# The cross stage's LayerNorm and the third quarter of the mix, turned by DMA in 16-bit planes

## The chip, the cores and the metric

One core of one Trainium2 chip. The metric is the device time of one execution in microseconds; the median of the runs counts. The engines are named as in the profile: PE (TensorE), DVE (VectorE), ACT (ScalarE), POOL (GpSimd) and SP (SyncE, which issues most DMAs). Each engine works through its own queue in order.

## The reference, cut to what matters

One layer of an encoder block over 256 tokens of width 2048, all in float32: a SwiGLU feed-forward, a mixer with two attentions, a cross attention to 256 memory tokens, and a second feed-forward, each followed by a LayerNorm. The change lies between the mixer's output and the cross attention's queries:

```python
# in the mixer: y_a, y_b are the two attentions' outputs, g_a and g_b the gates
return (g_a * y_a + g_b * y_b) @ w_out
# in the layer
h = layer_norm(ALPHA * h + mix, ln_mix_g[l], ln_mix_b[l])
xa = memory_cross_attention(h, mem, mem_ln_g[l], mem_ln_b[l], w_xq[l], w_xkv[l], w_xo[l])
h = layer_norm(ALPHA * h + xa, ln_x_g[l], ln_x_b[l])
# in memory_cross_attention
m = layer_norm(mem, mem_ln_g, mem_ln_b)
q = (h @ w_xq).reshape(b, s, X_HEADS, X_HEAD_DIM)
kv = (m @ w_xkv).reshape(b, m_len, 2, X_HEADS, X_HEAD_DIM)
```

## The kernel before

The 256 tokens are two token tiles of 128 (tt 0 and 1). Activations that enter a matmul are kept transposed, with the features on the partitions, as two halves: a high part (a copy rounded to the format that PE multiplies fast, fp32r) and a low part (the rest). `Act` holds them in blocks of 512 features, a "quarter" each. A product is computed as high x high + high x low + low x high.

Weights come in tiles of 1 MB. SP loads one into a `raw` buffer (three of them, L191); ACT casts its high part in two pieces (L262), DVE takes the low part (L265); two pairs of such buffers (`hi`, `lo`) are filled in turn while PE works on the other. A raw buffer is free again when its low part is taken. `run` writes this out: ahead of each item of the program it forms the tiles of the items to come, and `weave` puts side items (functions that form, send or join something) in front of given main items. A scheduler then places the instructions of each engine in one fixed order.

There are two ways to turn a [tokens x 512 features] piece.

- On PE: four transposes by the identity into PSUM (L417 in `ln_T`, L1301 in the mix).
- By DMA in 16-bit planes: `planes` (L840, ACT) separates the upper and lower 16 bits of each word into two planes, `send` (L844, SP) transposes both by one DMA, `join` (L848, ACT) puts the words together again. `issue_after` binds a send behind the last weight load issued, and a weight load behind the last send.

After either, `split` forms the high part (L253, ACT) and the low part (L254, DVE).

The stages around the change, in order:

- **w_o_b**, second half: `out_b(1)` multiplies by the gates and adds the two branches (L1275 to L1277, DVE), features 1024 to 1535 first (n = 0, the mix's third quarter), then 1536 to 2047 (n = 1, the fourth).
- **w_out**, two groups of eight steps. Step c (counted from 1 in this text) reads features 256(c-1) to 256c-1, so the third quarter is first read by the fifth step, the fourth by the seventh. PE does 24 matmuls of width 512 a step. Beside it runs `mem_norm`, the memory's LayerNorm: statistics on DVE (L387 to L399), a spread by eight small matmuls (L1365), and four quarters.
- **Cross stage, keys**: eight keys, one 1 MB tile each: 16 matmuls of width 512 (L275) and 16 of 256 (L277); ACT and DVE add and split the result (L283, L284, L253, L254). Beside them the LayerNorm of h: `ln_scale`, then `ln_T` on the quarters: scaling (L409 on DVE, L411 on ACT), four PE transposes, gain and bias out of PSUM (L424 on ACT, L426 on DVE), split.
- **Cross stage, queries**: two groups of eight steps over the same h, quarter 0 in steps 1 and 2, both token tiles in each step; the fifth and seventh steps of the first group work on sums of blocks (`forms_step`, `Sums`), whose weights use the blocks X2 and X3.

Of the kernel before, what the change touches and what calls it, by code (L numbers as in the profile page):

```python
# [13 lines left out]
AF = mybir.ActivationFunctionType  # L14
ALU = mybir.AluOpType
# [3 lines left out]
P = 128  # L19
# [80 lines left out]
class Kernel:  # L100
# [738 lines left out]
    def planes(self, s, u, n):  # L839
        return self.nc.scalar.copy(self.words(u, n).rearrange("p (k c) -> p k c", k=2),  # L840
                                   self.words(s, n).rearrange("p (c k) -> p k c", k=2))

    def send(self, s, u, n):
        return self.nc.sync.dma_start_transpose(self.words(s, n).rearrange("p (b q) -> p b q", q=P), self.words(u, n))  # L844

    def join(self, s, u, n, behind=None):
        with self.tc.issue_after((behind or self.next_hi).ins):
            self.nc.scalar.copy(self.words(u, n).rearrange("p (c k) -> p k c", k=2),  # L848
                                self.words(s, n).rearrange("p (k c) -> p k c", k=2))
# [14 lines left out]
    def mixer(self, xT, st, steps):  # L864
        nc, t = self.nc, self.t
        SPANS = ((0, P), (P, 3 * P))
        e = self.__dict__
# [26 lines left out]
        a, b, c = steps(1)  # L894
# [6 lines left out]
        bias = {}  # L901
# [303 lines left out]
        for i in range(NA):  # L1205
            side = [[lat_send(0)], [], [lat_join(0)], [lat_join(1)]][2 * i:2 * i + 2] if i < 2 else ([], [])
# [42 lines left out]
        n = B_HEADS - 1  # L1249
# [17 lines left out]
        def out_b(g):  # L1267
            ps, qs = {}, {}

            def done():  # L1270
                for n in range(2):
                    v = gates[2 * g + n]
                    for tt in range(2):
                        s = qs["add"][tt, n]
                        nc.vector.tensor_tensor(s, s, ps[tt, n], ALU.add)  # L1275
                        nc.vector.tensor_tensor(v[:, tt, 1, :], v[:, tt, 1, :], s, ALU.mult)
                    nc.vector.tensor_tensor(v[:, :, 1, :], v[:, :, 1, :], v[:, :, 0, :], ALU.add)  # L1277
                    if g == 0 or n:
                        for tt in range(2):
                            self.planes(v[:, tt, 1, :], v[:, tt, 0, :], 512)  # L1280

            def send(n):
                def fn():
                    for tt in range(2):
                        v = gates[2 * g + n][:, tt]
                        with self.tc.issue_after(self.last_load.ins):
                            self.sent = self.send(v[:, 1, :], v[:, 0, :], 512)
                return fn

            def turn(n, sent=True):  # L1290
                def fn():
                    mix.blocks += self.act([("X0", "X1", "T0", "X3")[2 * g + n]]).blocks
                    for tt in range(2):
                        v = gates[2 * g + n][:, tt]
                        if sent:
                            self.join(v[:, 1, :], v[:, 0, :], 512)
                            p = v[:, 0, :]
                        else:
                            p = self.group_tile(g)
                            for j in range(4):  # L1300
                                nc.tensor.transpose(p[:, j * P:(j + 1) * P], v[:, 1, j * P:(j + 1) * P], self.ident)  # L1301
                        hi, lo = (mix.blk(a, 8 * g + 4 * n, 4)[:, :, tt * P:(tt + 1) * P] for a in (0, 1))
                        self.split(p.rearrange("p (j q) -> p j q", j=4), hi, lo)
                return fn
            self.pair_group(g, t["w_o_b"][g], 512, KT, lambda: oB["t"], AT_YB[g], fb, ps, qs, None,
                            (("H5", "X2"), "X3"))
            self.add(done, prio=SOON)
            if g:
                return {2: [turn(0, False)], 3: [send(1)], 5: [turn(1)]}
            return {2: [send(0)], 4: [send(1)], 5: [turn(0)], 6: [turn(1)]}  # L1310

        main = self.collect(lambda: out_a(0))
# [4 lines left out]
        side = out_b(0)  # L1317
# [7 lines left out]
        side = self.mem_norm()  # L1325
# [54 lines left out]

        return {0: [load], 3: [stat], 7: [spread], 8: [quarter(0)], 10: [quarter(1)], 12: [quarter(2)], 14: [quarter(3)]}

    def cross(self, xT, st, steps, steps_out):
# [115 lines left out]
        form_q = lambda c: self.forms_step(fq, SUMS_XQ, c, xT)  # L1499
# [16 lines left out]
        a, b = steps(0), steps(1)  # L1516
        group(keys, {0: a[0] + b[0], 2: a[1], 4: a[2], 6: b[1], 8: b[2]}, 0, 8)
        side = group(query, {1: [form_q(4)], 3: [form_q(6)], 6: [form_q(2)]}, 0)
        side = group(query, both(side, {4: [form_v(2)]}), 1)
        group(val, both(side, {2: [form_v(4)], 4: [form_v(6)]}), 0)  # L1520
        group(keys, {0: [ready(0)], 2: [scores(0), gb(0)], 3: [send(0), ready(1)], 4: [gb(1)], 5: [join(0), scores(1)],
# [40 lines left out]
    def build(self):  # L1562
        self.setup()
        xT0, ps0 = self.start()
        x = {"T": xT0}
        xT = lambda: x["T"]
        st = [None, None]
        ln = [self.ln_steps(n, st, x) for n in ("ln_ffn1", "ln_mix", "ln_x")]
        self.ffn("ffn1", xT, st, ps0, ln[0], tags=(
            ("T0", "T1", "early"), ("T2", "T3", "early"), ("X0", "X1", "early"), ("X2", "X3", "early")))  # L1570
        self.mixer(xT, st, ln[0])
        self.cross(xT, st, ln[1], ln[2])
        load, fin = self.final_steps(st)
# [124 lines left out]
```

## Time and profile before

| | |
|---|---|
| runs, median (lowest, highest) | 2436.84 us (2436.31, 2438.87) |
| the profiled execution | 2436.7 us, its span 2434.9 us |
| granted PE clock, mean | 0.999 |
| PE busy | 99% of the span |
| DMA | 513.57 MB, mean 211 GB/s |

A row of the page or of the timeline names start and length in us, the engine, the line, the operation, out<-in with sizes, the count, and in brackets how long the engine had been idle and for whom. In the windows, each engine's busy time and count stand in the order PE, PE weight load, DVE, ACT, POOL, then the granted clock, the DMA share and GB/s. Grouped rows end in total busy time, mean ns of one, idle time ahead and who ended it. DMA rows end in the time from issue to landing.

### The profile page before, as it was taken

The page shows a single profiled execution, that of the slowest core. Times are in us where ns is not written, and L with a number is a line of the kernel's source. Part 1 is how long each engine was busy: PE and PEld are TensorE (multiplying, and loading weights), DVE is VectorE, ACT ScalarE, POOL GpSimd, SP SyncE. Part 2 cuts the span into 40 slices and gives each one's busy share as a digit, 9 for nine tenths or more (in the row PEclk, how much of TensorE's full clock was granted, in tenths as well). Part 3 has the DMA queues.
Part 4 walks back from the last instruction along what each step waited for, and adds up shares of the span by engine and source line. Part 5 has one row for each costly group of instructions (what it writes and reads, how often), then busy time and mean ns, then how long its engine had stood idle before and what let it go on. Part 6 is the DMA issues. An engine that isn't in the chain of part 4 may idle for free.

```text
span 2434.9 us, 29728 instructions
## 1 busy us (share of the span) xinstructions
PE 2420.7 (99%) x11314; PEld 2024.9 (83%) x11314; DVE 2120.0 (87%) x2428; ACT 1534.3 (63%) x2002; POOL 38.9 (2%) x83
## 2 busy tenths in 40 slices
PE   9999999999999999999999999999999999999998
PEld 8888888888888888888888888888888888888886
DVE  8999989899878897789789888879879999898996
ACT  6676745666555557878565667665666675557662
POOL 0000000000000001000000000000000000000000
PEclk9999999999999999999999999999999999999999
DMA  7766656667655657776576557655556666666664
GB/s 268 252 214 215 208 199 218 213 198 222 228 176 206 212 210 241 235 202 175 188 256 230 190 190 209 214 185 190 188 200 217 227 221 208 223 209 206 205 215 174
DMA packets 165854, 513.57 MB, mean 211 GB/s; under 512 B 101168, under 2 KB 101936, under 8 KB 110544
## 3 DMA queue, kind: packets, MB, share of 16 engines
q1 hardware_dynamic: 160256, 493.20, 61.0%
q0 software_dynamic: 4592, 17.30, 2.2%
q8 instruction: 88, 1.44, 0.2%
q10 hardware_dynamic: 864, 1.18, 0.1%
q14 instruction: 54, 0.44, 0.1%
HBM read 485.30 MB, written 2.10 MB: 200 GB/s over the span
## 4 chain that ended last, share of the span: by engine, by line
PE 91%; DVE 4%; ACT 3%; DMA 1%; issue 1%; SPq 0%; DVEq 0%; ACTq 0%
PE at L309 25%; PE mm L309 25%; PE at L363 11%; PE mm L363 11%; PE mm L296 10%; PE mm L275 5%; PE mm L277 2%; DVE lo L265 2%; ACT hi L262 1%; PE at L1027 1%; DMA raw<-w_xv 0%; PE at L417 0%; DMA raw<-w_xq 0%; PE at L1081 0%; ACT H L848 0%
## 5 line engine op out<-in xcount | busy, mean ns | idle before, releaser
L262 ACT CAST hi<-raw 128x1024 fp32r<-128x1024 f32 (+1 forms) x852 | 805.1, 982 | 473.8 <-PE at L309 160.2
L265 DVE TENSOR_TENSOR lo<-raw,hi 128x2048 fp32r<-128x2048 f32 (+1 forms) x427 | 902.2, 2114 | 139.6 <-ACT hi L262 134.4
L309 PE MATMUL mm<-hi,T 128*128 128x512 f32 (+1 forms) x1328 | 310.7, 383 | 0.2 <-ACT hi L253 0.2
L309 PEld LDWEIGHTS mm<-hi,T 128*128 128x128 f32 x1328 | 247.1, 188 | 47.1 <-ACT hi L253 0.7
L262 ACT CAST X<-H 128x1024 fp32r<-128x1024 f32 (+1 forms) x170 | 175.0, 1035 | 162.7 <-DVE H L246 126.2
L309 PE MATMUL at<-hi,T 128*128 128x512 f32 x1152 | 275.5, 389 | 0.0
L309 PEld LDWEIGHTS at<-hi,T 128*128 128x128 f32 x1152 | 216.2, 188 | 45.1
L265 DVE TENSOR_TENSOR X<-H,X 128x2048 fp32r<-128x2048 f32 (+1 forms) x85 | 191.4, 2251 | 66.3 <-ACT X L262 65.2
L309 PE MATMUL mm<-lo,T 128*128 128x512 f32 (+1 forms) x664 | 160.4, 382 | 0.0
L309 PEld LDWEIGHTS mm<-lo,T 128*128 128x128 f32 x664 | 123.7, 188 | 22.8
L309 PE MATMUL at<-lo,T 128*128 128x512 f32 x576 | 142.4, 389 | 0.0
L309 PE MATMUL at<-hi,H 128*128 128x512 f32 x560 | 133.7, 389 | 0.0
L309 PEld LDWEIGHTS at<-lo,T 128*128 128x128 f32 x576 | 108.1, 188 | 22.5
L309 PEld LDWEIGHTS at<-hi,H 128*128 128x128 f32 x560 | 104.9, 188 | 21.5
L248 DVE TENSOR_TENSOR H<-H,raw 128x512 f32<-128x512 f32 (+1 forms) x170 | 115.1, 677 | 2.2
L309 PE MATMUL mm<-hi,H 128*128 128x512 f32 x480 | 115.2, 391 | 0.1
L246 DVE TENSOR_TENSOR H<-raw 128x1024 f32<-128x1024 f32 (+1 forms) x85 | 101.9, 1199 | 4.8 <-DMA raw<-w_gate 4.4
L309 PEld LDWEIGHTS mm<-hi,H 128*128 128x128 f32 x480 | 89.6, 188 | 18.8 <-DVE w L284 0.5
L363 PE MATMUL mm<-X,X 128*128 128x512 f32 x342 | 91.1, 392 | 0.0
L363 PE MATMUL at<-X,X 128*128 128x512 f32 (+1 forms) x315 | 82.3, 385 | 0.4 <-ACT X L262 0.4
L262 ACT CAST X<-raw 128x1024 fp32r<-128x1024 f32 (+1 forms) x50 | 51.1, 1034 | 45.5 <-DVE raw L248 34.7
L848 ACT COPY w<-w 128x1024 uint16<-128x1024 uint16 (+1 forms) x60 | 75.7, 1275 | 1.4 <-DMA w<-w 1.4
(355 smaller groups left out, 4098.0 us busy)
## 6 DMA issues: line engine op xcount, KB each, us to landing
raw<-ffn_w_in SPq DMA_DIRECT2D x150, 1024.0 KB, 4.8
raw<-ffn_w_out SPq DMA_DIRECT2D x66, 1024.0 KB, 4.9
raw<-w_gate SPq DMA_DIRECT2D x32, 1024.0 KB, 4.9
raw<-ffn_w_out_r SPq DMA_DIRECT2D x16, 1024.0 KB, 5.0
raw<-w_qk SPq DMA_DIRECT2D x16, 1024.0 KB, 5.4
raw<-w_o_b SPq DMA_DIRECT2D x16, 1024.0 KB, 4.8
raw<-w_out SPq DMA_DIRECT2D x16, 1024.0 KB, 4.8
raw<-w_xk SPq DMA_DIRECT2D x16, 1024.0 KB, 4.9
```

What stands on the lines that cost most here:

```text
L246: self.nc.vector.tensor_tensor(two[0], two[1], raw[:, :m].unsqueeze(1).to_broadcast([P, 2, m]), ALU.add)
L248: self.nc.vector.tensor_tensor(t[:, a * m:a * m + m], t[:, b * m:b * m + m], raw[:, a * m:a * m + m], ALU.add)
L262: self.last_hi = self.nc.scalar.copy(hi[:, c:d], src[:, c:d])
L265: self.last_lo = self.nc.vector.tensor_tensor(lo[:, :n], src, hi[:, :n].bitcast(F32), ALU.subtract)
L275: self.nc.tensor.matmul(ps, hi[j], x.both(kt), start=(j == 0), stop=False)
L277: self.last_mm = self.nc.tensor.matmul(ps[:, :S], lo[j], x.at(0, kt), start=False, stop=(j == n - 1))
L296: self.last_mm = self.nc.tensor.matmul(ps, x.at(xi, kt)[:, tt * P:(tt + 1) * P], w[wi][:, j * 512 + c:j * 512 + c + m], start=(start and j ...
L309: self.last_mm = self.nc.tensor.matmul(ps[tt, g][:, :n], x.at(xi, kt)[:, tt * P:(tt + 1) * P], w[wi][:, c:c + n], start=first and j + wi + ...
L363: self.last_mm = self.nc.tensor.matmul(bank[:, :m], a[xi], v[wi][:, c * m:(c + 1) * m], start=own and first and wi + xi == 0, stop=own and ...
L848: self.nc.scalar.copy(self.words(u, n).rearrange("p (c k) -> p k c", k=2), self.words(s, n).rearrange("p (k c) -> p k c", k=2))
L1027: nc.tensor.matmul(ps[:, c0:c0 + nk], q[:, tt * P:(tt + 1) * P], k[:, :nk], start=(j == 0), stop=(j == len(parts) - 1))
```

## The change

The third quarter of the mix no longer goes through PE: `planes`, `send`, `join` and `split` serve all four quarters. The cross stage's LayerNorm no longer uses `ln_steps`; a new `turned_norm` gives four kinds of steps (scale, planes, send, join), which are spread over the eight keys and the first steps of the first query group. Its planes live in the blocks X2, X3, H5 and X2 again.

```diff
@@ out_b, done
-                    if g == 0 or n:
-                        for tt in range(2):
-                            self.planes(v[:, tt, 1, :], v[:, tt, 0, :], 512)
+                    for tt in range(2):
+                        self.planes(v[:, tt, 1, :], v[:, tt, 0, :], 512)
@@ out_b, turn
-                        if sent:
-                            self.join(v[:, 1, :], v[:, 0, :], 512)
-                            p = v[:, 0, :]
-                        else:
-                            p = self.group_tile(g)
-                            for j in range(4):
-                                nc.tensor.transpose(p[:, j * P:(j + 1) * P], v[:, 1, j * P:(j + 1) * P], self.ident)
+                        self.join(v[:, 1, :], v[:, 0, :], 512)
...
             if g:
-                return {2: [turn(0, False)], 3: [send(1)], 5: [turn(1)]}
+                return {1: [send(0)], 3: [turn(0), send(1)], 5: [turn(1)]}
@@
+    def turned_norm(self, ln, st, x):
+        nc, e, got = self.nc, {}, {}
+        def scale(tt):
+            def fn():
+                if tt == 0:
+                    x["T"] = self.act(["T0", "T1", "T2", "T3"])
+                got[tt] = self.ln_scale(st[tt])
+            return fn
+        def planes(tt, q):
+            def fn():
+                if q % 2 == 0:
+                    e[tt, q // 2] = self.block(("X2", "X3", "H5", "X2")[2 * tt + q // 2], (P, 2, 2, 512))
+                mean, r, nb = got[tt]
+                hs = self.h[tt][:, q * 512:(q + 1) * 512]
+                nc.vector.tensor_scalar(hs, hs, mean, r, ALU.subtract, ALU.mult)
+                self.planes(hs, e[tt, q // 2][:, q % 2, 0, :], 512)
+            return fn
+        def send(tt, q):
+            def fn():
+                v = e[tt, q // 2][:, q % 2]
+                with self.tc.issue_after(self.last_load.ins):
+                    self.sent = self.send(v[:, 1, :], v[:, 0, :], 512)
+            return fn
+        def join(tt, q):
+            def fn():
+                v = e[tt, q // 2][:, q % 2]
+                self.join(v[:, 1, :], v[:, 0, :], 512)
+                f, a = (v[:, i, :].rearrange("p (j c) -> p j c", j=4) for i in range(2))
+                for j in range(4):
+                    kt = 4 * q + j
+                    g, b = self.vec(ln + "_g", kt), self.vec(ln + "_b", kt)
+                    if j % 2 == 0:
+                        nc.scalar.activation(a[:, j], f[:, j], AF.Identity, bias=b, scale=g)
+                    else:
+                        nc.vector.tensor_scalar(a[:, j], f[:, j], g, b, ALU.mult, ALU.add)
+                self.split(a, *(x["T"].blk(s, 4 * q, 4)[:, :, tt * P:(tt + 1) * P] for s in (0, 1)))
+            return fn
+        return scale, planes, send, join
@@ cross
-        a, b = steps(0), steps(1)
-        group(keys, {0: a[0] + b[0], 2: a[1], 4: a[2], 6: b[1], 8: b[2]}, 0, 8)
-        side = group(query, {1: [form_q(4)], 3: [form_q(6)], 6: [form_q(2)]}, 0)
+        scale, planes, nsend, njoin = norm
+        group(keys, {0: [scale(0), scale(1)], 1: [planes(0, 0), planes(0, 1)], 2: [nsend(0, 0), nsend(0, 1), planes(0, 2)],
+                     3: [planes(0, 3), nsend(0, 2), njoin(0, 0)], 4: [nsend(0, 3), njoin(0, 1), planes(1, 0)],
+                     5: [planes(1, 1), nsend(1, 0), njoin(0, 2)], 6: [nsend(1, 1), njoin(0, 3), planes(1, 2)],
+                     7: [planes(1, 3), nsend(1, 2), njoin(1, 0)], 8: [nsend(1, 3), njoin(1, 1)]}, 0, 8)
+        side = group(query, {1: [njoin(1, 2)], 2: [form_q(4), njoin(1, 3)], 4: [form_q(6)], 6: [form_q(2)]}, 0)
@@ build
-        self.cross(xT, st, ln[1], ln[2])
+        self.cross(xT, st, self.turned_norm("ln_mix", st, x), ln[2])
```

How it moves the instructions is seen at three places. The first is DVE at the start of w_out. `lo` with its buffers is a weight's low part (the last one shown is that of w_out's fifth step, loaded into raw_10382 before and raw_10371 now), BN_STATS and BN_AGGR are the memory's statistics, and the L254 on a T block is the third quarter's low part. Before:

```order
L265 TENSOR_TENSOR lo_10339<-raw_10336,hi_10338 128x2048
L254 TENSOR_TENSOR T_1626_10343<-at_10344,T_1626_10343 128x4x128
L254 TENSOR_TENSOR T_1626_10343<-at_10351,T_1626_10343 128x4x128
L265 TENSOR_TENSOR lo_10385<-raw_10382,hi_10384 128x2048
L387 BN_STATS bn_10392<-T_1612_10269 128x6 x4
L387 BN_STATS bn_10415<-T_1613_10270 128x6
```

Now, to the first token tile's low part:

```order
L265 TENSOR_TENSOR lo_10374<-raw_10371,hi_10373 128x2048
L387 BN_STATS bn_10381<-T_1612_10271 128x6 x4
L387 BN_STATS bn_10404<-T_1613_10272 128x6
L392 BN_AGGR mv_10386<-bn_10381 128x2
...
L387 BN_STATS bn_10404<-T_1613_10272 128x6
L375 TENSOR_SCALAR a_10389<-y_10388,v_10387 128x1
L392 BN_AGGR mv_10409<-bn_10404 128x2
L254 TENSOR_TENSOR T_1647_10431<-H_970_6445,T_1647_10431 128x4x128
```

The quarter's low parts moved from ahead of the fifth step's low weight to behind it and behind all eight statistics.

The second is SP from the third key's load on. Before, the loads of keys (w_xk) and queries (w_xq) follow one another:

```order
L191 DMA raw_10986<-w_xk 128x2048
L191 DMA raw_11031<-w_xk 128x2048
L191 DMA raw_11106<-w_xk 128x2048
L191 DMA raw_11151<-w_xk 128x2048
L191 DMA raw_11223<-w_xk 128x2048
L191 DMA raw_11268<-w_xk 128x2048
```

Now:

```order
L191 DMA raw_11036<-w_xk 128x2048
L844 DMA_TRANSPOSE X_1716_10993<-X_1716_10993 128x8x128 x2
L191 DMA raw_11086<-w_xk 128x2048
L844 DMA_TRANSPOSE X_1722_11045<-X_1722_11045 128x8x128
L191 DMA raw_11141<-w_xk 128x2048
L844 DMA_TRANSPOSE X_1722_11045<-X_1722_11045 128x8x128
L191 DMA raw_11198<-w_xk 128x2048
L844 DMA_TRANSPOSE H_1733_11156<-H_1733_11156 128x8x128
L191 DMA raw_11253<-w_xk 128x2048
```

Two transposes stand ahead of the fifth key's load (raw_11086), one ahead of each load after it.

The third is PE at the first query step, whose first token tile goes to the banks mm_11379 and mm_11380, the second to mm_11381 and mm_11382; T_1696 is quarter 0. Before (mm_11417 and mm_11418 are the first token tile's banks, the other two the second's):

```order
L417 MATMUL at_11405<-ident,h_102 128x128 x4
L309 MATMUL mm_11417<-hi_11341,T_1719_11038 128x512 [waits Activation_49]
L309 MATMUL mm_11417<-hi_11341,T_1719_11038 128x512
L309 MATMUL mm_11418<-hi_11341,T_1719_11038 128x512 [waits DVE_49,PE_49]
L309 MATMUL mm_11418<-hi_11341,T_1719_11038 128x512
L309 MATMUL mm_11419<-hi_11341,T_1719_11038 128x512 [waits DVE_49]
```

Now:

```order
L309 MATMUL mm_11379<-hi_11311,T_1696_10911 128x512 [waits Activation_49]
L309 MATMUL mm_11379<-hi_11311,T_1696_10911 128x512
L309 MATMUL mm_11380<-hi_11311,T_1696_10911 128x512 [waits PE_49]
L309 MATMUL mm_11380<-hi_11311,T_1696_10911 128x512
L309 MATMUL mm_11379<-hi_11311,T_1696_10911 128x512 [waits Activation_49]
L309 MATMUL mm_11379<-hi_11311,T_1696_10911 128x512
L309 MATMUL mm_11380<-hi_11311,T_1696_10911 128x512
L309 MATMUL mm_11381<-hi_11311,T_1696_10911 128x512 [waits Activation_49]
```

Seven matmuls of the first token tile now stand ahead of the first one of the second, which waits for ACT; the LayerNorm's transposes are gone. On ACT the joins of the second token tile's first two quarters stand together behind the last plane copy, then the last key's total (L283), then the split of quarter 0.

More of the change, by code (lines that the diff above doesn't have):

```diff
@@ L1288, in send, with turn @@
                 return fn
-            def turn(n, sent=True):
+            def turn(n):
                 def fn():
@@ L1294, in fn @@
                         v = gates[2 * g + n][:, tt]
-                        if sent:
-                            self.join(v[:, 1, :], v[:, 0, :], 512)
-                            p = v[:, 0, :]
-                        else:
-                            p = self.group_tile(g)
-                            for j in range(4):
-                                nc.tensor.transpose(p[:, j * P:(j + 1) * P], v[:, 1, j * P:(j + 1) * P], self.ident)
+                        self.join(v[:, 1, :], v[:, 0, :], 512)
                         hi, lo = (mix.blk(a, 8 * g + 4 * n, 4)[:, :, tt * P:(tt + 1) * P] for a in (0, 1))
-                        self.split(p.rearrange("p (j q) -> p j q", j=4), hi, lo)
+                        self.split(v[:, 0, :].rearrange("p (j q) -> p j q", j=4), hi, lo)
                 return fn
@@ L1381, in mem_norm, with cross @@
         return {0: [load], 3: [stat], 7: [spread], 8: [quarter(0)], 10: [quarter(1)], 12: [quarter(2)], 14: [quarter(3)]}
-    def cross(self, xT, st, steps, steps_out):
+    def turned_norm(self, ln, st, x):
[36 more added lines that the diff above has]
+        return scale, planes, send, join
+    def cross(self, xT, st, norm, steps_out):
         nc, t, e = self.nc, self.t, self.mem
```

## The prediction

> **What bounds the kernel now.** The first view is the page's busy shares and the chain that ended last.
>
> ```profile
> PE 2420.7 (99%) x11314; PEld 2024.9 (83%) x11314; DVE 2120.0 (87%) x2428; ACT 1534.3 (63%) x2002; POOL 38.9 (2%) x83
> PE 91%; DVE 4%; ACT 3%; DMA 1%; issue 1%; SPq 0%; DVEq 0%; ACTq 0%
> ```
>
> TensorE is busy for 2420.7 of 2434.9 us. Every matmul removed there is worth its length, as long as nothing else makes TensorE wait; every wait that is added counts in full. The second view is the windows over the two stages that the change touches, the start of w_out and the first eight keys of the cross stage.
>
> ```profile
> 1290.00:1330.00 40.00, 40.00 (x186) 33.33 (x185) 34.81 (x54) 21.05 (x24) 0.00 (x0) 1.00 0.68 217
> 1374.00:1422.00 48.00, 47.97 (x289) 42.48 (x287) 39.77 (x74) 31.50 (x55) 0.00 (x0) 1.00 0.52 178
> ```
>
> TensorE (first column) never stops in either. VectorE works 87% and 83% of them, ScalarE 53% and 66%. So there is room on ScalarE, but not much on VectorE. The third view is the chain in order of time, where the transposes stand among the matmuls.
>
> ```profile
> 1285.06 10.88 PE mm L309 x48
> 1295.94 0.87 PE at L1301 x8
> 1296.82 27.23 PE mm L309 x120
> ...
> 1373.91 3.63 PE mm L275 x16
> 1377.54 1.91 PE mm L277 x16
> ...
> 1385.02 0.44 PE at L417 x4
> ...
> 1385.96 0.66 PE at L417 x4
> ...
> 1397.30 0.87 PE at L417 x8
> ...
> 1421.33 0.87 PE at L417 x8
> 1422.21 21.81 PE mm L309 x96
> ```
>
> A 512-wide matmul takes 27.23/120 = 0.227 us, a w_out step of 24 of them 5.44, a key 3.65 + 1.92 = 5.57.
>
> **What leaves.** The mix's eight transposes: 0.87 us. The LayerNorm's 32: without them the first query step would start at 1373.91 + 8 x 5.57 = 1418.47 instead of 1422.21, so 3.74 us. Together 4.61 us, or 2432.1 against the profiled execution's 2436.7, if nothing waits. (That execution's span is 2434.9; the median of the runs is 2436.8, so differences carry over with +0.1.)
>
> **The mix's third quarter.** It now goes through ScalarE (two plane copies), SP (two transposes), ScalarE (two joins, two splits) and VectorE (two low parts). The rows of w_out's first half:
>
> ```profile
> 1295.86 1.21 DVE L1277 TENSOR_TENSOR H<-H 128x1024 f32<-128x1024 f32 x1
> 1302.59 2.29 DVE L265 TENSOR_TENSOR lo<-raw,hi 128x2048 fp32r<-128x2048 f32 x1 [1.67 <-ACT hi L262]
> 1304.80 3.06 DVE L387 BATCH_NORM_STATS2 bn<-T 128x6 f32<-128x512 f32 x5
> 1310.38 2.23 DVE L265 TENSOR_TENSOR lo<-raw,hi 128x2048 fp32r<-128x2048 f32 x1
> 1313.15 0.68 DVE L254 TENSOR_TENSOR X<-H,X 128x512 fp32r<-128x512 f32 x1
> 1297.11 2.00 ACT L840 COPY H<-H 128x1024 uint16<-128x1024 uint16 x2 [0.94 <-DVE H L1277]
> 1299.01 1.07 ACT L253 CAST T<-at 128x512 fp32r<-128x512 f32 x2
> 1308.98 2.56 ACT L848 COPY H<-H 128x1024 uint16<-128x1024 uint16 x2
> 1311.41 1.13 ACT L253 CAST X<-H 128x512 fp32r<-128x512 f32 x2
> 1312.45 2.00 ACT L262 CAST hi<-raw 128x1024 fp32r<-128x1024 f32 x2
> ```
>
> From start to start a plane copy costs ScalarE 0.95 us, a join 1.22, a split 0.52, a weight tile 1.9. VectorE's low part of a weight costs 2.2.
>
> The order on VectorE is what decides. Before, the third quarter's low parts stood ahead of the low weights of w_out's fifth step and of the memory's statistics (L387 to L392). Now they stand behind both. I follow that piece. The fourth quarter's plane copies start when L1277 ends, at 1297.1, and end at 1299.0; that VectorE chain is unbroken and unmoved. The fourth step's weight tile, which used to be cast ahead of them, now follows them: 1300.9. Then the first join, 1302.1, and the fifth step's weight tile, 1304.0. VectorE takes that tile's low part until 1306.3, then the eight statistics with their small steps, which before ran from 1304.80 to 1310.38, 5.58 us: 1311.9. Only then comes the quarter's first low part, 0.6: 1312.5. TensorE reaches the fifth step at 1307.70 - 0.87 = 1306.83, has four matmuls that need the high part only (0.9), and waits from 1307.7 to 1312.5, 4.8 us. Before, it stood at that point at 1308.6. Net +3.9; one of the spread's eight matmuls (0.1) is pulled into the gap: **+3.8 us** for this half. What it rests on: the weights must be there. In the queue the fourth and fifth steps' loads now stand behind two transposes; those can start at 1290.8 (planes behind the first half of a weight tile), leave SP at 1293.3, and a load behind two transposes took this long:
>
> ```profile
> 1298.18 2.72 SPq L844 DMA_TRANSPOSE H<-H  x2
> raw<-w_out SPq DMA_DIRECT2D x1, 1024.0 KB, 6.0
> ```
>
> That gives 1299.3 for the fourth step's tile and about 2 us more for the fifth's, just ahead of their casts. Bounds for this half: +3.4 (no join ahead of the tile) to +6 (the loads 2 us later). Nothing is late behind it: the sixth step's tile lands by 1309, its low part is done at 1316.3, and TensorE wants it at 1316.8 + 3.6.
>
> **The LayerNorm.** Each of eight quarters is now scaled on VectorE alone (L409's op; the four L411 on ScalarE go), copied to planes, sent, joined, multiplied by gain and bias from SBUF instead of PSUM, and split. ScalarE gains 8 x (0.95 + 1.22) and loses 4 x 0.7: +14.6 us in a stretch where it had 16.5 us free, and it takes its queue in order. So I add up that queue as the order gives it.
>
> ```profile
> 1383.19 2.00 ACT L262 CAST hi<-raw 128x1024 fp32r<-128x1024 f32 x2 [1.97 <-PE mm L275]
> 1385.09 0.81 ACT L411 ACTIVATE h<-h,nb,y 128x512 f32<-128x512 f32 x1
> L283 ACT COPY w<-mm 128x256 f32<-128x256 f32 x69 | 24.6, 367 | 9.1 <-PE mm L277 9.0
> L253 ACT CAST X<-w 128x256 fp32r<-128x256 f32 x16 | 6.5, 405 | 17.0 <-DVE w L284 17.0
> L424 ACT ACTIVATE w<-at,vecs 128x128 f32<-128x128 f32 x48 | 20.6, 456 | 5.2 <-PE at L417 4.1 <-DVE w L426 0.6
> w<-w SPq DMA_TRANSPOSE x60, 3.1
> 1469.28 5.27 DMA raw<-w_xq
> ```
>
> (Times on the clock of before.) ScalarE is free for the first planes at 1385.1; the copy ends at 1386.1, the transpose lands 3.1 us later, and the first join starts at 1389.3, ScalarE having waited 1.9 us for it. From there to the split that completes quarter 0 of the second token tile stand six joins (7.3), six plane copies (5.7), five weight tiles (9.5), six key totals and six key splits (0.3 each with the 0.1 by which neighbours overlap: 3.5), twelve gain-and-bias steps (0.36: 4.3) and five splits (2.6): 32.9 us, so 1422.2. Two things lengthen it. The load of the fifth key's tile stands behind two transposes, leaves at 1388.8 and takes 5.3: 1394.1, 0.4 us late for ScalarE; the next tile waits a little too. And a step that reads what the step ahead of it wrote loses some 0.1. I add 1.6: 1423.8. TensorE ends the keys at 1418.47, has seven matmuls of the first token tile to do (1.6: 1420.0), and then waits **3.8 us** for that split. Bounds: 2 (no waits) to 7. The keys themselves get through: the fifth key's first half tile is ready at 1395.1, wanted at 1396.2. VectorE's part lies beside this, its low part 0.7 us after the split, under four matmuls. At no cost I put the four scalings that move to VectorE (0.5 each, in 8 us of free time there; without that room they would delay the low weights by 2) and the ten further transfers (256 KB each, at a DMA share of 0.52 in this window). Later quarters are joined at 1430 and 1431 and wanted four steps on. Net for the LayerNorm: 3.8 - 3.74 = **+0.1**.
>
> One rule speaks against the change. The rows give 0.87 us for eight transposes on TensorE and 3.1 for a whole transfer, eight blocks of 128x128 in 16 bits. The Trainium skill ("VectorE: DVE Perf Modes", section "The three transpose paths") puts one such block at 1309 ns by DMA and 390 ns on TensorE and advises TensorE where PSUM will do. Eight blocks end to end would be, as an estimate from that page, 10.5 us a transfer, and the first join 7 us later; the trace's 3.1 does not agree, so the sum goes by the row.
>
> **The sum:** +3.8 + 0.1 = 3.9; 2436.8 + 3.9 = **2440.7 us**, 0.16% slower, which counts as no change (0.2%, 4.9 us, is about what can be told here).
>
> **The rivals.** (B) *Transposes land late between loads*: on the slower side.
>
> ```profile
> H<-H SPq DMA_TRANSPOSE x6, 7.8
> ```
>
> In the mix stage transposes set between loads took 7.8 us; in the key stage each now stands between two loads. If the first took that, the first join and all behind it come 4.7 us later, first as a wait at the fifth key (tile ready at about 1399.8 instead of 1396.2), the rest at the query: 2440.7 + 4.7 = 2445.4. It decides from 1.0 us of lateness on (2441.7). Against it: the queue is empty when the first one goes. (C) *ScalarE keeps up*: its bursts have slack, the LayerNorm's 3.74 come in whole, and only the mix's wait stays: 2436.8 + 3.8 - 3.7 = 2436.9. Against it the 32.9 us above. (D) *Both are hidden*: 2432.2; it needs the statistics done 5 us sooner in the mix, and the order sets them behind a low weight that cannot start before 1304.0. (E) *The wait costs clock*:
>
> ```profile
> 2418.12 5.03 PE L296 MATMUL mm<-X,H 128*128 128x512 f32 x30
> 2427.50:2428.00 0.50, 0.00 (x0) 0.00 (x0) 0.50 (x1) 0.00 (x0) 0.50 (x2) 0.91 0.00 0
> 2428.00:2429.00 1.00, 0.00 (x0) 0.00 (x0) 1.00 (x2) 0.00 (x0) 1.00 (x2) 0.50 0.00 0
> ```
>
> After the last matmul (2423.2) the granted clock holds 4.7 us and then falls to 0.50. A wait as long, followed by the fifth step's last 20 matmuls at half speed, costs 20 x 0.227 = 4.5 us: 2445.2. The spread's matmul breaks this wait in two, which speaks against it. The Trainium skill ("TensorE: Matmul & The Clock Gate", section "What's actually happening") has the clock halve after one idle window of about 3.4 us; by that rule the second wait (3.8) could do it too, and the trace agrees that some such limit exists.
>
> **How the numbers follow.** A 0.50 (its own range 2438.5 to 2443, of which 0.13 lies over 2441.7), B 0.27, C 0.13, D 0.06 (0.04 of it faster), E 0.04. Slower 0.13 + 0.27 + 0.04 = 0.44, faster 0.04, the same 0.52. The range takes in C below and most of B and E above: 2434.5 to 2447.5.
>
> **What would show it.** TensorE's busy time falls by 4.6 to about 2416, its idle time grows by some 8.5. In w_out's fifth step TensorE waits 4 to 5 us for VectorE's L254, right behind the statistics; at the first query step 2 to 5 us for ScalarE's L253. ScalarE is over 85% busy between the first planes and the query. I am wrong if the fifth step of w_out shows no wait, if the keys wait for weights, or if a transpose of the key stage lands in over 5 us.

## The result, and the profile after

| | before | after |
|---|---|---|
| runs, median (lowest, highest) | 2436.95 us (2436.31, 2438.87) | 2446.92 us (2444.71, 2450.21) |
| the profiled execution, its span | 2436.7, 2434.9 us | 2444.71, 2442.8 us |
| granted PE clock, mean | 0.999 | 0.996 |

The ratio is 1.0039, with a 95% interval of 1.0029 to 1.005: slower, by more than the 0.2% that can be told. The forecast of 2440.7 us was 6.2 us too low.

The page after the change, its busy shares and its chain:

```profile
PE 2421.1 (99%) x11274; PEld 2023.7 (83%) x11274; DVE 2121.4 (87%) x2432; ACT 1553.4 (64%) x2018; POOL 38.8 (2%) x83
PE 94%; ACT 2%; DVE 1%; DMA 1%; issue 1%; SPq 0%; DVEq 0%; ACTq 0%
```

The forty transposes are gone (11314 instructions before, 11274 now), yet TensorE is busy for as long as before. So the others took longer. The view of TensorE's waits has three new rows at its top:

```profile
PE mm L309 <- ACT T L253: 3.9, 1, 3.9
PE at L1358 <- DVE y L371: 2.5, 1, 2.5
PE mm L309 <- DVE T L254: 1.3, 1, 1.3
```

**In w_out.** The timeline of TensorE and then of VectorE, in the fifth step:

```profile
1306.94 1.07 PE L309 MATMUL mm<-hi,T 128*128 128x512 f32 x4
1310.48 0.77 PE L1358 MATMUL at<-w,w 128*128 128x128 f32 x2 [2.46 <-DVE y L371]
1312.59 5.11 PE L309 MATMUL mm<-hi,T 128*128 128x512 f32 x12 [1.34 <-DVE T L254]
```

```profile
1304.11 2.29 DVE L265 TENSOR_TENSOR lo<-raw,hi 128x2048 fp32r<-128x2048 f32 x1 [0.82 <-ACT hi L262]
1306.32 3.06 DVE L387 BATCH_NORM_STATS2 bn<-T 128x6 f32<-128x512 f32 x5
1311.91 0.63 DVE L254 TENSOR_TENSOR T<-H,T 128x512 fp32r<-128x512 f32 x1
```

Low weight, statistics, and only then the quarter's low part, as worked out; TensorE goes on at 1312.59 (predicted 1312.5), with two of the spread's matmuls in the gap. What was not in the sum stands in the third row: twelve matmuls take 5.11 us. By before's 0.227 each they take 2.7.

**In the cross stage.** TensorE, then ScalarE's first join and the split that TensorE waits for, then the transposes and the keys' loads:

```profile
1424.46 1.78 PE L309 MATMUL mm<-hi,T 128*128 128x512 f32 x7
1430.16 1.65 PE L309 MATMUL mm<-hi,T 128*128 128x512 f32 x3 [3.92 <-ACT T L253]
```

```profile
1395.65 1.37 ACT L848 COPY X<-X 128x1024 uint16<-128x1024 uint16 x1 [2.10 <-DMA X<-X]
1429.48 0.62 ACT L253 CAST T<-H 128x512 fp32r<-128x512 f32 x1
```

```profile
raw<-w_xk SPq DMA_DIRECT2D x5, 1024.0 KB, 5.8
X<-X SPq DMA_TRANSPOSE x6, 3.1
```

Seven matmuls, then 3.9 us of waiting for the split of quarter 0 of the second token tile. No key waits. Three matmuls then take 1.65 us, again twice too long.

**The clock.** Cut at the right places, the windows of the same trace show it. The columns are the stretch, its length, the busy time of TensorE, the weight loads, VectorE, ScalarE and GpSimd, then the granted clock, DMA share and GB/s:

```profile
1306.88:1310.29 3.41, 1.13 (x6) 0.59 (x4) 3.41 (x10) 2.79 (x3) 0.00 (x0) 1.00 0.92 339
1310.29:1313.71 3.42, 1.89 (x5) 1.43 (x6) 3.42 (x15) 2.62 (x4) 0.00 (x0) 0.50 0.54 230
1313.71:1317.12 3.41, 3.41 (x10) 2.64 (x9) 3.41 (x12) 0.00 (x0) 0.00 (x0) 0.50 0.05 7
1426.34:1429.76 3.42, 0.00 (x0) 0.00 (x0) 2.50 (x7) 3.42 (x6) 0.00 (x0) 1.00 0.97 242
1429.76:1433.17 3.41, 3.01 (x7) 2.44 (x8) 2.23 (x4) 3.32 (x6) 0.00 (x0) 0.50 0.97 404
```

The clock fell at 1310.29 and came back at 1317.12, fell at 1429.76 and came back at 1433.17. 6.83 is 2 x 3.413, 3.41 is one, and from 1310.29 to 1429.76 there are 35.0 of them. So the changes lie on a grid, and it looks as if the clock is set at the end of each of its windows by how busy TensorE was in it: 1.13 of 3.41 us was too little to keep it, 1.89 too little to get it back.

**Where the 7.9 us of the span went.** Three marks of the chain, the start of w_out, the first key and the first step of the query's sums, after the change:

```profile
1285.35 3.64 PE mm L309 x16
1380.11 3.63 PE mm L275 x16
1452.05 0.91 PE mm L363 x4
```

Before, w_out began at 1285.06 and the first key at 1373.91, and the sums began here:

```profile
1444.02 0.91 PE mm L363 x4
```

From w_out to the keys it took 94.76 us instead of 88.85, **+5.9**; from there to the sums 71.94 instead of 70.11, **+1.8**; 0.3 stood ahead of w_out already. Of the 5.9, half speed on the work from 1312.59 to 1317.12 is (4.53 / 2) 2.3, and 3.6 is the net of the wait (predicted 3.8). Of the 1.8, half of the 3.01 us is 1.5, and 0.3 the net of wait and transposes (predicted 0.1). The profiled execution is the fastest of the five; where the 2.2 us by which the median lies above it went, no trace shows.

### The profile page after: what moved, and what is told of

Read it like the earlier page. It is cut to its first block, busy times and chain, and to the rows that moved or that the text cites. A ratio compares the mean times of both kernels' runs of the same rounds, so it can differ in the third digit from the quotient of the medians.

```text
span 2442.8 us, 29692 instructions
## 1 busy us (share of the span) xinstructions
PE 2421.1 (99%) x11274; PEld 2023.7 (83%) x11274; DVE 2121.4 (87%) x2432; ACT 1553.4 (64%) x2018; POOL 38.8 (2%) x83
## 4 chain that ended last, share of the span: by engine, by line
PE 94%; ACT 2%; DVE 1%; DMA 1%; issue 1%; SPq 0%; DVEq 0%; ACTq 0%
PE at L309 26%; PE mm L309 25%; PE at L363 11%; PE mm L363 11%; PE mm L296 10%; PE mm L275 4%; PE mm L277 2%; PE at L1027 1%; ACT hi L262 1%; PE at L1494 0%; PE at L275 0%; PE at L1081 0%; DMA raw<-w_xq 0%; PE at L417 0%; ACT w L826 0%
## 5 line engine op out<-in xcount | busy, mean ns | idle before, releaser
L265 DVE TENSOR_TENSOR lo<-raw,hi 128x2048 fp32r<-128x2048 f32 (+1 forms) x427 | 902.3, 2115 | 140.9 <-ACT hi L262 134.7
L265 DVE TENSOR_TENSOR X<-H,X 128x2048 fp32r<-128x2048 f32 (+1 forms) x85 | 191.3, 2251 | 66.3 <-ACT X L262 66.3
```

The lines of the kernel that those rows point to most:

```text
L265: self.last_lo = self.nc.vector.tensor_tensor(lo[:, :n], src, hi[:, :n].bitcast(F32), ALU.subtract)
```

## The experiments

The theory: the order on VectorE and the queue of ScalarE each make TensorE wait once, and what the prediction lacks is the clock, which both waits let fall. A ratio whose interval holds 1 can't be told from no change. Each kernel was timed beside the kernel before, and the ratios are to it. Its median was 2437.64 us beside the two halves, the filled kernel and the early statistics, 2436.91 beside the half-filled kernel, the gain on VectorE, the order by quarter and both orders, and 2437.42 beside the last three.

**Each half alone.** The mix's part of the diff on the kernel before, and the cross stage's part on it.

> The mix's third quarter goes by DMA, the cross stage's LayerNorm stays on TensorE as before. Theory (the order on VectorE makes the fifth step of w_out wait, and the wait lets the clock fall at the end of a fixed window of about 3.4 us): from the trace of the full change, the keys started 6.20 us later, of which 0.29 stood ahead of w_out, so +5.9: 2442.8 us. If the windows of the clock lie elsewhere in a run, between 2440.7 (no fall) and 2444. The trace shows TensorE waiting for L254 behind the statistics, nothing new in the keys. Rival (the two halves need each other: the cross stage costs only because the mix has delayed it, or the extra transfers of both fight): under +3 or over +8.

Measured: 2445.42 us, ratio 1.0031 (1.0019 to 1.0042), +7.8. The profiled execution had 2444.09; counted from the start of w_out the keys began 6.4 us late, with these rows:

```profile
1310.55 0.46 PE L1358 MATMUL at<-w,w 128*128 128x128 f32 x2 [2.62 <-DVE y L371]
1312.66 5.46 PE L309 MATMUL mm<-hi,T 128*128 128x512 f32 x12 [1.66 <-DVE T L254]
```

```profile
1307.76:1311.17 3.41, 0.63 (x3) 0.30 (x2) 3.41 (x11) 3.41 (x4) 0.00 (x0) 1.00 0.99 353
1311.17:1314.58 3.41, 1.92 (x5) 1.53 (x6) 3.41 (x13) 2.00 (x3) 0.00 (x0) 0.50 0.26 111
1314.58:1318.00 3.42, 3.42 (x10) 2.65 (x9) 3.41 (x10) 0.00 (x0) 0.00 (x0) 0.50 0.25 41
```

The same wait, and two windows at half clock. The median lies 1.4 us over the bound that the theory gave (2444); the interval reaches down to it, so this neither bears out nor refutes the size, and it reaches beyond the +8 at which the rival begins.

> The cross stage's LayerNorm goes by DMA, the mix's third quarter stays on TensorE as before. Theory: 3.74 us of transposes leave, 3.9 us of waiting for ScalarE come, and the clock falls once for some 3.4 us, which costs up to 1.7: from the trace of the full change +1.8, so 2438.7 us, and between 2437.0 (no fall) and 2440.5. TensorE waits at the first query step for L253 of the second token tile's first quarter. Rival (transposes between loads land late, and the keys pay): a wait in the keys and +4 or more. Rival (the halves are not independent): the wait at the query is gone, because without the shift of the mix the transfers meet other loads: 2433.

Measured: 2438.62 us, ratio 1.0004 (0.9995 to 1.0013), near the theory's 2438.7; neither rival. The interval holds 1. In the profiled execution (span 2437.3) the wait was 3.15 us and the clock did not fall:

```profile
1424.54 0.96 PE L309 MATMUL mm<-hi,T 128*128 128x512 f32 x3 [3.15 <-ACT T L253]
```

```profile
1419.42:1422.84 3.42, 1.97 (x10) 1.32 (x9) 3.03 (x4) 3.42 (x5) 0.00 (x0) 1.00 0.86 307
1422.84:1426.25 3.41, 1.72 (x7) 1.43 (x8) 2.14 (x5) 3.41 (x8) 0.00 (x0) 1.00 1.04 281
```

Where the windows end is taken here from the fall after the last matmul, at 2429.77, counted back in steps of 3.413. The wait lies across a boundary, both windows have over 1.7 us of work, and three matmuls take 0.96 us. The two halves cost +7.8 and +1.0; the full change +10.0. So nearly all of the loss is the mix's, the half with 0.87 us of transposes to win.

**The clock alone.** The full change, and in each wait TensorE multiplies a weight tile by itself: n is 18 in w_out's fifth step, behind its first four matmuls, and 16 in the first query step, behind the first token tile's eight; in the half-filled kernel 9 and 8.

```diff
+p = self.at_tile()
+for _ in range(n):
+    with self.tc.issue_after(self.last_mm.ins):
+        self.last_mm = self.nc.tensor.matmul(p, w[0][:, :P], w[0][:, :512], start=True, stop=True)
```

> The full change, and in each of the two waits TensorE multiplies something whose result nobody reads: 18 matmuls of width 512 in the fifth step of w_out, 16 in the first query step, fixed in place behind the matmuls that can run and ahead of those that wait. Theory (idle time alone makes the clock fall): 18 x 0.227 = 4.1 us and 16 x 0.227 = 3.6 us lie inside the waits, so nothing is lost by them; the granted clock stays at 1.00 through both places, the 12 and the 16 matmuls behind them take 0.23 us each again, and 2.1 + 1.7 = 3.8 us come back: 2443.1 us against 2446.9 of the full change. The runs of one kernel also spread less. Rival (the half clock has another cause, such as the start of work after any wait for another engine, or the transfers): the clock falls all the same, 2447 or more. Rival (the clock costs nothing beside the waits): no difference.

Measured: 2443.44 us, ratio 1.0022 (1.0013 to 1.0031): +5.8 where the full change has +10.0. All eleven runs (2442.23 to 2444.09) lie below the fastest of the full change (2444.71).

```profile
1308.83 4.24 PE L318 MATMUL at<-hi 128*128 128x512 f32 x18
1313.88 3.10 PE L308 MATMUL mm<-hi,T 128*128 128x512 f32 x12 [0.81 <-DVE T L254]
```

The twelve take 3.10 us instead of 5.11, and the clock stayed at 1.00 through both places. The data came no sooner. So some 4 of the 10 us are the clock's by the medians, and idleness is its cause; both rivals fall. In the two traces it is 3.0: from the start of w_out to the query's sums it took 163.73 us here and 166.70 in the full change. With the gaps filled 4.8 us are still lost there against before's 158.96, and the forecast had 3.9 for both waits, net; what makes up the rest is not shown.

> The full change, with half as many matmuls that nobody reads: 9 in the fifth step of w_out, 8 in the first query step, at the start of each wait. Some 2.5 and 2.1 us of the waits stay idle. Theory (the clock falls at the end of a fixed window of 3.4 us that was nearly or for two thirds idle; in the full change one with 1.05 us of work in it still let it fall): idle stretches this short hardly ever fill two thirds of a window, the clock stays at 1.00 in nearly all executions, 2443.5 us as with all the matmuls. Rival (any idle stretch over some 2 us makes it fall): 2445 to 2447 and a fall in the trace.

Measured: 2444.9 us (2444.51 to 2445.82), ratio 1.0033 (1.0021 to 1.0046), +8.0: next to the rival's 2445 and not at the theory's 2443.5. The trace shows the fall that the rival asked for, once, in w_out:

```profile
1308.61:1312.02 3.41, 1.22 (x6) 0.59 (x4) 3.41 (x13) 3.41 (x5) 0.00 (x0) 1.00 0.87 351
1312.02:1315.44 3.42, 3.33 (x8) 2.65 (x9) 3.42 (x10) 1.07 (x3) 0.00 (x0) 0.50 0.00 0
```

My bound of two thirds idle was too high: 1.22 of 3.41 us of work (36%) is still too little. (The window of the full change that I put at 1.05 us has 1.13.) In this trace no stretch of waiting was over 1.7 us, and two of them in one window were enough.

**The order on VectorE.** The full change, the memory's statistics two steps earlier, where VectorE had been idle for 4.2 us.

```diff
-return {0: [load], 3: [stat], 7: [spread], 8: [quarter(0)], 10: [quarter(1)], 12: [quarter(2)], 14: [quarter(3)]}
+return {0: [load], 1: [stat], 7: [spread], 8: [quarter(0)], 10: [quarter(1)], 12: [quarter(2)], 14: [quarter(3)]}
```

> The full change, with the memory's statistics two steps of w_out earlier: they stand on VectorE ahead of the fourth step's low weights, in the 4.2 us in which VectorE had nothing to do (1296.8 to 1301.0). Theory (the order on VectorE is what made the fifth step wait): L254 ends at about 1307.5 instead of 1312.5, just ahead of TensorE's need at 1307.7; no wait in w_out and no fall of the clock there; the mix gives -0.87 instead of +5.9, so 2446.9 - 6.8 = 2440.1 us. The wait at the query stays. Rival (the fifth step waits for its weights, which stand in SP's queue behind two transposes, or for the joins): TensorE still waits 3 us or more there, for L265 or L253, and the time falls by less than 2.

Measured: 2439.94 us, ratio 1.0011 (1.0002 to 1.002), 0.2 from the theory. TensorE's wait in w_out's fifth step is down to this row:

```profile
1308.12 1.66 PE L309 MATMUL mm<-hi,T 128*128 128x512 f32 x6 [0.59 <-DVE T L254]
```

So the place of eight statistics on VectorE held 4 us of wait and all of the clock's loss in w_out. The wait at the query stayed, 3.11 us, and the clock fell there for two windows. That the time meets the theory is partly luck: in the trace the stretch from w_out to the query's sums is 5.2 us shorter than the change's, not 6.8. The 0.87 us of the transposes did not come in (88.95 us from w_out to the keys, before 88.85), and the fall at the query lasted one window longer than in the change.

**ScalarE's queue.** The cross stage's half alone (mix as before), first with the gain and bias of all blocks on VectorE, then with the steps in another order: quarter by quarter for both token tiles.

```diff
-if j % 2 == 0:
-    nc.scalar.activation(a[:, j], f[:, j], AF.Identity, bias=b, scale=g)
-else:
-    nc.vector.tensor_scalar(a[:, j], f[:, j], g, b, ALU.mult, ALU.add)
+nc.vector.tensor_scalar(a[:, j], f[:, j], g, b, ALU.mult, ALU.add)
```

> The cross stage's LayerNorm by DMA in the change's own order, the mix as before, but all four gain-and-bias blocks of a quarter on VectorE instead of two on ScalarE. Theory (the length of ScalarE's queue ahead of the split is the wait): twelve steps of 0.36 us leave that queue, 4.3 us against a wait of 3.1 to 3.9; the wait falls under 1 us, and the time to 2437.6 - 3.74 + 0.5 = 2434.4 us. Rival (VectorE, which gets two steps of 0.3 us a quarter more and must deliver the gain before the split, is as late): the wait stays over 2 us, for a split that itself waits for VectorE, 2437 or more.

Measured: 2436.6 us, ratio 0.9996 (0.9987 to 1.0005). The split came in time, at 1418.28, ahead of the query at 1419.09. But another wait took the place:

```profile
1418.28 0.61 ACT L253 CAST T<-H 128x512 fp32r<-128x512 f32 x1
```

```profile
1419.09 1.09 PE L309 MATMUL mm<-hi,T 128*128 128x512 f32 x4
1420.91 2.36 PE L309 MATMUL mm<-hi,T 128*128 128x512 f32 x8 [0.72 <-DVE w L284]
1425.61 1.20 PE L309 MATMUL mm<-hi,T 128*128 128x512 f32 x4 [1.66 <-DVE w L284]
```

L284 empties the PSUM bank of a key, and the query's accumulators stand in the same four banks. Neither theory nor rival had that: ScalarE's queue did set the split, and behind its wait another was hidden. That the bank is what this wait is for is shown further down, where other banks remove it.

```diff
-group(keys, {0: [scale(0), scale(1)], 1: [planes(0, 0), planes(0, 1)], 2: [nsend(0, 0), nsend(0, 1), planes(0, 2)],
-             3: [planes(0, 3), nsend(0, 2), njoin(0, 0)], 4: [nsend(0, 3), njoin(0, 1), planes(1, 0)],
-             5: [planes(1, 1), nsend(1, 0), njoin(0, 2)], 6: [nsend(1, 1), njoin(0, 3), planes(1, 2)],
-             7: [planes(1, 3), nsend(1, 2), njoin(1, 0)], 8: [nsend(1, 3), njoin(1, 1)]}, 0, 8)
-side = group(query, {1: [njoin(1, 2)], 2: [form_q(4), njoin(1, 3)], 4: [form_q(6)], 6: [form_q(2)]}, 0)
+group(keys, {0: [scale(0), scale(1)], 1: [planes(0, 0), planes(1, 0)], 2: [nsend(0, 0), nsend(1, 0), planes(0, 1)],
+             3: [planes(1, 1), nsend(0, 1), njoin(0, 0)], 4: [nsend(1, 1), njoin(1, 0), planes(0, 2)],
+             5: [planes(0, 3), nsend(0, 2), njoin(0, 1)], 6: [nsend(0, 3), njoin(1, 1), planes(1, 2)],
+             7: [planes(1, 3), nsend(1, 2)], 8: [nsend(1, 3), njoin(0, 2)]}, 0, 8)
+side = group(query, {1: [njoin(1, 2)], 2: [form_q(4), njoin(0, 3), njoin(1, 3)], 4: [form_q(6)], 6: [form_q(2)]}, 0)
```

> The cross stage's LayerNorm by DMA, the mix as before, and the order of the steps changed: for each quarter both token tiles, where the change takes all four quarters of the first token tile ahead of the second's. The work is the same. Theory (ScalarE takes its queue in order, and what the first query step waits for stands behind work for later steps): quarter 0 of the second token tile is split four keys earlier, TensorE does not wait at the first query step, the clock stays at 1.00 there, and the 3.74 us of transposes come in whole: -3.7, 2433.9 us against a kernel before of 2437.6. Rival (ScalarE is over-full as such, the wait moves to the third query step or to the sums): TensorE waits 2 to 4 us at another place of the first query group, 2436 to 2438. Rival (the keys' weights now come late, since four plane copies stand together ahead of a tile): a wait in the keys.

Measured: 2435.59 us, ratio 0.9999 (0.999 to 1.0008), less than the theory's -3.7. The wait for the split is gone without moving any work to another engine; 0.41 us at the fifth key and 1.5 us for the bank remain:

```profile
1396.33 3.94 PE L275 MATMUL mm<-H,hi 128*128 128x512 f32 x16 [0.41 <-ACT hi L262]
1421.76 2.56 PE L309 MATMUL mm<-hi,T 128*128 128x512 f32 x10 [1.49 <-DVE w L284]
```

**Towards a version that gains.** First this order together with the early statistics.

> The full change with the memory's statistics two steps earlier and the cross stage's steps by quarter. Theory: no wait at either place, so the 4.61 us of transposes come in whole: -4.6, 2433.0 us. Rival (one wait stays or a new one comes): 2435 or more.

Measured: 2436.78 us, ratio 1.0 (0.9991 to 1.0009): the rival. Three waits stayed in its trace, 0.58 for L254, 0.42 at the fifth key, 1.15 for the bank. Then each was taken up:

```diff
-ps = self.at_tile() if j in (8, 9, 10) else self.mm_tile()
+ps = self.at_tile() if j in (6, 7, 8, 9, 10) else self.mm_tile()
```

> As the run by quarter (mix as before), and the seventh and eighth key accumulate in the PSUM banks that the transposes no longer use. Theory (in the run by quarter the first query step waited 1.5 us for L284, which frees the bank of the last key; the four accumulators of the query stand in the same four banks as the keys): that wait is gone, the matmuls of the query start at once, and of the 3.74 us all but the 0.4 us at the fifth key come in: 2436.9 - 3.3 = 2433.6 us. Rival (another wait ends just behind it: the low part of the first quarter or the second weight tile of the query): TensorE still waits over 1 us in the first two query steps, 2435 or more.

Measured: 2435.76 us, ratio 0.9995 (0.9987 to 1.0004). The bank's wait is gone:

```profile
1419.90 3.82 PE L309 MATMUL mm<-hi,T 128*128 128x512 f32 x16
```

From the first key (1374.41) to the query's sums (1441.68) it took 67.27 us, 2.8 less than before's 70.11. But the sums then waited 0.75 us for a low weight, and the span ends level with before's at 2434.9. The runs' median gained 1.7 us, half of what was expected.

```diff
-return {0: [load], 3: [stat], 7: [spread], 8: [quarter(0)], 10: [quarter(1)], 12: [quarter(2)], 14: [quarter(3)]}
+return {0: [load], 1: [stat(0)], 4: [stat(1)], 7: [spread], 8: [quarter(0)], 10: [quarter(1)], 12: [quarter(2)], 14: [quarter(3)]}
```

> The mix's third quarter by DMA, the cross stage as before, and the memory's statistics in two parts: those of the first memory tile ahead of the fourth step's low weights, those of the second behind the sixth step's. Theory (with all eight of them early, the fourth step's low weights came 0.2 us late and L254 0.6): both waits are under 0.2 us and the transposes' 0.87 us come in: 2436.9 - 0.7 = 2436.2 us. Rival (the joins and the loads behind the transposes set it, and the order on VectorE no more): L254 still makes TensorE wait 0.5 us, no gain: 2437.

Measured: 2437.83 us, ratio 1.0003 (0.9994 to 1.0011): the rival's time. With only half of the statistics in front, L254 is late by as much as with all:

```profile
1308.90 3.74 PE L309 MATMUL mm<-hi,T 128*128 128x512 f32 x15 [0.61 <-DVE T L254]
```

```profile
1302.44 1.36 ACT L848 COPY H<-H 128x1024 uint16<-128x1024 uint16 x1
1303.67 1.99 ACT L262 CAST hi<-raw 128x1024 fp32r<-128x1024 f32 x2
```

On ScalarE a join stands ahead of the fifth step's weight tile, and on VectorE that tile's low part (1305.68 to 1307.89) stands ahead of L254 (1308.16). Which of the two orders holds L254 up is not shown: the split that it needs ended at 1306.17 already, so L254 ahead of the low part is a remedy that was not tested. From the fifth step's first matmul (1307.90) to the sixth's (1314.29) it took 6.39 us instead of 5.44, so all of the 0.87 us went again.

> The full change with all three edits: the statistics in two parts, the cross stage's steps by quarter, the last two keys in free banks. Theory: -0.7 and -3.3 add up, 2436.9 - 4.0 = 2432.9 us. Rival (a gain of one is taken back by the other, or the clock falls at a place where it did not): 2434 or more.

Measured: 2435.19 us (2434.7 to 2437.78), ratio 0.9993 (0.9984 to 1.0002). It beats the change (1.0039) and is the lowest median of all, but its interval still holds 1. In its trace the query's first step begins 2.9 us sooner than before's, and 2.4 of that go again by the end, in waits of 0.3 to 0.5 us far behind the change, as here:

```profile
PE at L363 <- DVE X L265: 0.9, 2, 0.5
PE at L417 <- DVE h L409: 0.5, 1, 0.5
```

Whether the gain brings these about or executions simply differ by as much is not settled: the 27 runs of the kernel before in this group span from 2436.16 to 2443.37 us. One thing speaks against the gain: the trace of the early statistics, which reached the query's sums 2.3 us later than before's, has the wait for L409 too (1.07 us, at 1743.29; here at 1738.50), and the later of the two for L265 (0.51 us, at 2052.51; here at 2047.86).

## Why the prediction came out as it did

- **The mix's wait: right.** Place, cause and size hold: L254 behind the statistics, TensorE on again at 1312.59 against 1312.5. With the statistics moved away the wait shrank from 4 us to 0.6.
- **The LayerNorm's wait: right.** ScalarE's queue summed up to 1423.8 on before's clock; the split ended at 1430.1, which is 1423.9 less the shift of the keys (6.2). The wait was 3.9 against 3.8. ScalarE was busy for 35.10 of the 38.81 us between the first planes and the split, 90%.
- **The step that failed: rival E, the wait that costs clock, at 0.04.** I set it against one wait, and against that I held that the spread's matmul breaks the wait in two. The runs showed that this is no protection: what counts is the work in a fixed window of 3.41 us, and the spread's 0.77 us are too little. The 4.7 us that I read off the end of before's trace as the time for which the clock holds depended on where the windows lay: in the change's trace the clock fell 2.25 us after the last matmul (2431.03 and 2433.28). The half clock struck twice and cost 2.3 and 1.5 us in the profiled execution, where I had put one fall at 4.5; in the medians it is some 4 (the filled kernel). The Trainium skill ("TensorE: Matmul & The Clock Gate", section "What's actually happening") has a free-running window of 3413 ns; the traces agree (2 x 3.413 for the fall in w_out). It says that one idle window throttles; here windows with 1.13 and 1.22 us of work did too, which its sentence does not tell. I had that sentence, and left the second wait out of the sum.
- **What followed from it.** TensorE's busy time was to fall by 4.6 and stayed, since the matmuls at half clock take longer. "Within 0.2%" was given 0.52 and was wrong; the range held the time only near its upper end, and that is partly luck: the room up there was made for B, which did not come, and for one fall of the clock that I held unlikely.
- **Rival B (transposes late between loads): wrong as a cause.** The key stage's transposes landed in 3.1 us at the median. One, issued at 1400.6, took 6.3, over the 5 us that I had named as a sign of being wrong, yet no key waited, and ScalarE's next join did not wait for a transfer either.
- **Rivals C and D: wrong.** The traces show both waits.
- **Hidden behind the LayerNorm's wait: the PSUM banks.** Had ScalarE kept up, as C supposed, TensorE would still have waited 1.5 to 2.4 us for L284 (the runs by quarter and with the gain on VectorE). So C's 3.74 us were not to be had by that alone.

The removed work was worth 4.61 us on paper. The best arrangement found brings some 2 in the medians, in an interval that includes none.

## What to carry to other kernels

A wait on a TensorE that is otherwise full costs its length and, in these traces from about 2 idle microseconds in one window of 3.4 on (1.96 was too much, 1.69 was not), some 1.5 to 3.0 us of half clock behind it; matmuls that fill a third of the window do not save it, so the wait must be cut or the gap filled. When work leaves TensorE for an engine that takes its queue in order, sum up that queue up to each deadline and look for work without a near deadline that stands ahead; here moving eight statistics by two steps recovered 7.7 of 10.0 us, and changing the order of the same steps removed the other wait. Before counting a removed wait as gain, ask which condition would have ended second, here a PSUM bank.

## What the runs showed of the hardware

The clock's grid holds over an execution: in the profile of the change the falls at 1310.29 and at the very end, 2433.28, lie 329.0 windows of 3.413 us apart. The last matmuls there, and the windows at that fall:

```profile
2426.00 5.03 PE L296 MATMUL mm<-X,H 128*128 128x512 f32 x30
2429.87:2433.28 3.41, 1.17 (x10) 0.96 (x8) 3.17 (x10) 0.66 (x2) 0.00 (x0) 1.00 0.45 169
2433.28:2434.00 0.72, 0.00 (x0) 0.00 (x0) 0.61 (x5) 0.72 (x3) 0.57 (x1) 0.50 0.00 0
```

At the end of a window the clock fell after 0, 0.63, 1.13, 1.17, 1.22 and 1.45 us of TensorE work in it and held after 1.72 and 1.97; once down, it stayed down after 1.89, 1.92 and 2.53 us and rose after 3.01. The 1.45 is the last window at full clock of the filled kernel:

```profile
2428.95:2432.36 3.41, 1.45 (x13) 1.25 (x11) 3.17 (x10) 0.38 (x1) 0.00 (x0) 1.00 0.53 199
```

Another 1.17 and the 2.53 come from these windows of the change with early statistics:

```profile
1418.73:1422.14 3.41, 1.17 (x6) 0.62 (x4) 2.81 (x6) 3.41 (x6) 0.00 (x0) 1.00 1.12 362
1422.14:1425.55 3.41, 2.53 (x6) 2.05 (x7) 1.89 (x4) 3.41 (x8) 0.00 (x0) 0.50 0.89 308
```

So getting the clock back takes more busy time in a window than keeping it. That need not be a second threshold: at half clock a matmul is busy for nearly twice as long (twelve took 5.11 us where before's rate gives 2.7), so the 2.53 and the 3.01 are, as an estimate, some 1.3 and 1.5 to 1.6 us of work at full clock, and one threshold of work between 1.45 and that would fit every figure here. The runs do not tell the two apart.

Since the grid's place against the program differs between executions (the wait in w_out met a boundary at 1310.29 in one kernel's trace and at 1312.02 in another's), so does the cost. The spread of the runs is no measure of it: the five runs of the change span 5.5 us and the eleven of the filled kernel 1.9, but the five of the half-filled kernel, with a fall, span 1.3, and 27 runs of the kernel before span up to 7.2.
